# Two weight halves by DMA: a casting load for the rounded half, an accumulating load for the residual

## The chip, the cores and the metric

The kernel runs on one core of a Trainium2 chip. The metric is device time in microseconds of one execution of the whole program, the median of three runs. Below, TensorE is the matrix engine (PE in the profile, with PEld for its weight loads), VectorE is DVE, ScalarE is ACT, GpSimd is POOL and SyncE is SP. DMAs are issued from an engine's queue in the order in which they stand there; those of SyncE go to the hardware queue (q1), those of GpSimd to the software queue (q0).

## The reference

A two-layer decoder trunk for 512 tokens plus 16 learned meta tokens, width 1024, float32. Each sub-layer is `h = LayerNorm(alpha * h + f(h))`:

```
h = concat(meta, x)                                  # 528 tokens
layer 0: h = LN(a*h + gated_deltanet(h));   h = LN(a*h + conv_ffn(h))
layer 1: h = LN(a*h + short_conv_mixer(h)); h = LN(a*h + conv_ffn(h))
conv_ffn(h):         u, gate = split(h @ w_up);  (silu(conv3(u)) * gate) @ w_down     # d_ff 2816
short_conv_mixer(h): b, c, v = split(h @ w_in);  (b * conv3(c * v)) @ w_out
gated_deltanet(h):   q, k, v, z, beta, decay from h @ w_in, conv4 and silu;
                     chunked gated delta rule over 8 heads of 128; RMS norm; * silu(z); @ w_out
```

## The kernel before

Activations lie transposed, 128 channels on the partitions and tokens along the row: `h` holds 8 such slices of 528 tokens. Every large product runs in float32r with both operands in two parts: `hi`, the value rounded to float32r, and `lo`, the rest. A product `W x` is three TensorE products per 128x128 block, `hi*x_hi + hi*x_lo + lo*x_hi` (lines 174 to 176, in `mm_steps`).

Weights come in **strips**: 128 output channels by 1024 (or 768) inputs, a tile of 128 partitions x 1024 numbers, 512 KB. There are 208 of them, in the list `strips` in the order of their use: 24 for q, k and v of the delta net, 8 for its gate z, 8 for its output, then 168 for the first feed-forward (in three parts of 8, 8 and 6 blocks, each an `up` and a `down`), the short convolution (`w_bi`, `w_bo`) and the second feed-forward. `get()` hands out the next strip and first calls `prep` for the strips up to `look` ahead. `prep(i)` allocates a `raw` buffer and a buffer each for `whi` and `wlo`, loads the strip on SyncE's queue into `raw`, and splits it: ScalarE copies `raw` to `whi` with rounding (line 72), VectorE writes `wlo = raw - whi` (line 73). The rings have 4 `raw` buffers (`NR`) and 10 each of `whi` and `wlo` (`NW = (4, 6)`) once the second pool is open; in the delta-net stage 4 and 2. A buffer is written again only when the products that read it are done.

The program is written in one order, and a scheduler sets the final order on each engine's queue; each engine then works its queue strictly in order. The first part (mixer 0, the delta net) weaves the recurrences of the heads with the projections of later heads; there GpSimd also computes (`rk` at 361, `NT` at 380, `R` at 425, `ro` at 494, and others). From the mixer's output projection on (tiles `pd`), TensorE goes through `up` (tiles `pu`), `down` and `short_conv`, with six PSUM banks between it and the engines that empty them: ScalarE copies `pu` to `u` (752), VectorE convolves, ScalarE applies SiLU (756) and the split of the gated result makes `gh` and `gl` (again lines 72 and 73). GpSimd issues eight loads of `x` into `h` at line 568 and then has nothing more to do.

Of the kernel before, what the change touches and what calls it, by code (L numbers as in the profile page):

```python
# [8 lines left out]
F32 = mybir.dt.float32  # L9
# [3 lines left out]
AF = mybir.ActivationFunctionType  # L13
ALU = mybir.AluOpType
PSUM = bass.MemoryType.PSUM

P = 128
D = 1024
KD = D // P
# [38 lines left out]
def tile_hybrid_trunk(ctx, tc, xt, par, cst, msk, w_ba, w_qkv, w_z, w_ao, w_bi, w_bo, w_up, w_dn, out):  # L58
    nc = tc.nc
    V, S, G, TE = nc.vector, nc.scalar, nc.gpsimd, nc.tensor  # L60
# [6 lines left out]
    h = hpool.tile([P, KD, T], F32, name="h")  # L67
# [3 lines left out]
    def split(hi, lo, src):  # L71
        S.activation(hi, src, AF.Copy)  # L72
        V.tensor_tensor(lo, src, hi.bitcast(F32), ALU.subtract)  # L73

# [1 line left out]
    par_sb = cpool.tile([P, NPAR], F32, name="par_sb")  # L76
    cst_sb = cpool.tile([P, NCST], F32, name="cst_sb")
    msk_sb = cpool.tile([P, len(LEVELS), CH], U8, name="msk_sb")
# [8 lines left out]
    nc.sync.dma_start(ba_raw, w_ba)  # L87
    nc.sync.dma_start(h[:, 0, :], xt[:, 0, :])

    # strips of all weights, in the order of their use  # L90
    strips = []

    def add(w, idx, nk=KD, k0=0):
# [12 lines left out]
    SC_LEAD = ((0, 0), (0, 1), (1, 0), (1, 1), (2, 0), (2, 1))  # L106

    def order(nj, parts, lead):
        """(strip, part) in the order of their use."""
        return lead + tuple(x for x in ((j, p) for j in range(nj) for p in range(parts)) if x not in lead)  # L110

    def add_ffn(i):
# [6 lines left out]
    n_gdn = len(strips) - 8  # L119
    add_ffn(0)  # L120
    for j, part in order(8, 3, SC_LEAD):
        add(w_bi, (1, 2, 0)[part] * 8 + j)
# [3 lines left out]

    ready = []
    pools = [wpool]
    NW = (4, 6)
    NR = (2, 2)  # L130
    HOLD6, HOLD8 = 7, 5
    FFN_GRP, SC_GRP = (4, 2), (4, 2)
    STAG = 2
    OUTS = {1: 0, 3: 2, 5: 4, 6: 6, 7: 7}
    UB, CB = 4, 3

    def prep(i):
        src, nk = strips[i]
        x = 0 if i < n_gdn or (i - n_gdn) % sum(NW) < NW[0] else 1
        r = 0 if i < n_gdn + NW[0] or (i - n_gdn - NW[0]) % sum(NR) >= NR[1] else 1  # L140
        raw = pools[r].tile([P, KD, P], F32, name=f"raw{i}", tag="raw", bufs=NR[r])
        hi = pools[x].tile([P, KD, P], F32R, name=f"whi{i}", tag="whi", bufs=NW[x])
        lo = pools[x].tile([P, KD, P], F32R, name=f"wlo{i}", tag="wlo", bufs=NW[x])
        step = nk if i else 4
        for k in range(0, nk, step):
            nc.sync.dma_start(raw[:, k : k + step, :], src[:, k : k + step, :])
        for k in range(0, nk, step):
            split(hi[:, k : k + step, :], lo[:, k : k + step, :], raw[:, k : k + step, :])
        ready.append((hi, lo))

    state = {"next": 0, "look": 3}
# [1 line left out]
    def get():  # L153
# [3 lines left out]
        if len(pools) == 1:  # L157
            end = min(end, n_gdn + NW[0])
        while len(ready) < end:
# [51 lines left out]
    def bcm(ap, n):  # L211
        return ap.unsqueeze(1).to_broadcast([ap.shape[0], n, ap.shape[1]])

    # ================= mixer 0: gated delta net =================
    with ExitStack() as gctx:
        gp = gctx.enter_context(tc.tile_pool(name="gp", bufs=1))
        pm = gctx.enter_context(tc.tile_pool(name="pm", bufs=2, space=PSUM))
# [13 lines left out]
        def gbank(name, tag):  # L231
            return pg.tile([P, 4, P], F32, name=name, tag=tag, bufs=1)

# [1 line left out]
        ba_sb = gp.tile([16, TP], F32, name="ba_sb", tag="ba_sb")  # L235
        V.memset(ba_sb[:, T:], 0.0)
        psba = gtile("psba", 1).rearrange("p (b c) i -> p b (c i)", b=2)
# [11 lines left out]
        beta = cpool.tile([CH, NH, NC_], F32, name="beta")  # L249
# [74 lines left out]
        R5 = range(NC_)  # L324

        def outer(c32, c_hi, c_lo, mat, name, ch, eng):
            """[j, c, i] <- sum_t 1[t > j] mat[t, i] col[t, c]"""
            n = NC_ - 1
            b_hi = gp.tile([CH, n, CH], F32R, name=f"bh{name}", tag="B", bufs=2)
            b_lo = gp.tile([CH, n, CH], F32R, name=f"bl{name}", tag="B", bufs=2)  # L330
            b_32 = gp.tile([CH, CH], F32, name=f"bf{name}", tag="Bf", bufs=2)
            eng.tensor_tensor(b_hi, bcm(mat, n), bc(c_hi[:, :n].bitcast(F32), CH), ALU.mult)
            eng.tensor_tensor(b_lo, bcm(mat, n), bc(c_lo[:, :n], CH), ALU.mult)
            eng.tensor_scalar(b_32, mat, c32[:, n:], None, ALU.mult)
            ps = gtile(f"ps{name}", ch)
            TE.matmul(ps[:CH, :n, :CH], strict_r[:CH], b_hi, start=True, stop=False)
            TE.matmul(ps[:CH, :n, :CH], strict_r[:CH], b_lo, start=False, stop=True)
            TE.matmul(ps[:CH, n, :CH], strict, b_32, start=True, stop=True)
            return ps

        def gdn_a(hd, box, qT, kT, vT, PT):
            """Yields (time of its products, time until what they feed is ready)."""
            ch = hd % 2
            qTv, kTv, vTv = qv(qT), qv(kT), qv(vT)
            small = lambda nm, dt=F32: gp.tile([CH, NC_], dt, name=f"{nm}{hd}", tag=nm, bufs=3)
# [48 lines left out]
            V.tensor_tensor(NT, NT, ps[:CH, :NC_, :CH], ALU.mult)  # L394
            V.tensor_scalar(N16, NT, NSC, None, ALU.mult)
            yield 900, 2200
            # (I - N)^-1 by doubling of the diagonal blocks
            for li in range(len(LEVELS)):
                m_d = bcm(msk_sb[:CH, li, :], NC_)
                p1 = gtile(f"p1{hd}{li}", ch)  # L400
# [19 lines left out]
                S.activation(DT16, pt[:CH, :NC_, :CH], AF.Copy)  # L420
                if not last:
                    yield 250, 1500
            # two correction steps; the residual and its factor in two parts each
            R = full("R")
            G.tensor_tensor(R, D16, bcm(ident16[:CH, :CH], NC_), ALU.subtract)
            yield 250, 2000
# [22 lines left out]
        def gdn_b(hd, box):  # L449
            PT, DT, kd, vb, ssq, nbe, rk, qTv, kTv = (  # L450
                box[x] for x in ("PT", "DT", "kd", "vb", "ssq", "nbe", "rk", "qT", "kT"))
            vn = gp.tile([CH, NC_, P], F32, name=f"vn{hd}", tag="vn")
            oS = gp.tile([CH, NC_, P], F32, name=f"oS{hd}", tag="oS", bufs=1)
            St = gp.tile([P, P], F32, name=f"St{hd}", tag="St")
            rr = gp.tile([CH, P], F32, name=f"rr{hd}", tag="rr")
            sa = gbank(f"sa{hd}", "gb")
            sb = gbank(f"sb{hd}", "gc")
            for c in R5:
                r_ = vb[:, c, :]
                if c > 0:  # L460
                    TE.matmul(sa[:CH, 0, :], kTv[:, c, :], St, start=True, stop=True)
                    TE.matmul(sb[:CH, c - 1, :], qTv[:, c, :], St, start=True, stop=True)
                    V.scalar_tensor_tensor(rr, sa[:CH, 0, :], nbe[:, c : c + 1], vb[:, c, :], ALU.mult, ALU.add)
                    r_ = rr
                    yield 430, 600
                TE.matmul(sa[:CH, 1, :], DT[:, c, :], r_, start=True, stop=True)
                S.activation(vn[:, c, :], sa[:CH, 1, :], AF.Copy, scale=rk[:, c : c + 1])
                yield 220, 800
                if c < NC_ - 1:
                    TE.matmul(sa[:, 2, :], kd[:, c, :], vn[:, c, :], start=True, stop=True)  # L470
                    if c == 0:
                        V.tensor_copy(St, sa[:, 2, :])
                    else:
                        V.scalar_tensor_tensor(St, St, egl[:, hd, c : c + 1], sa[:, 2, :], ALU.mult, ALU.add)
                    yield 220, 800
            V.tensor_tensor(oS[:, 1:, :], sb[:CH], bc(eg[:, hd, 1:], P), ALU.mult)
            yield 0, 500
            ps = gbank(f"po{hd}", "gb")
            for c in range(1, NC_):
                TE.matmul(ps[:CH, c - 1, :], PT[:, c, :], vn[:, c, :], start=True, stop=True)  # L480
            V.tensor_tensor(oS[:, 1:, :], ps[:CH], oS[:, 1:, :], ALU.add)
            ps = gbank(f"po0{hd}", "gc")
            TE.matmul(ps[:CH, 0, :], PT[:, 0, :], vn[:, 0, :], start=True, stop=True)
            S.activation(oS[:, 0, :], ps[:CH, 0, :], AF.Copy)
            # RMS norm, q's length folded into its guard
            sq = gp.tile([CH, P], F32, name=f"sqb{hd}", tag="sqb")
            sso = gp.tile([CH, NC_], F32, name=f"sso{hd}", tag="sso", bufs=2)
            ro = gp.tile([CH, NC_], F32, name=f"ro{hd}", tag="ro", bufs=2)
            for c in R5:
                S.activation(sq, oS[:, c, :], AF.Square, accum_out=sso[:, c : c + 1])  # L490
            V.tensor_scalar(ssq, ssq, L2_EPS, RMS_EPS * P * P, ALU.add, ALU.mult)
            V.tensor_tensor(sso, sso, ssq, ALU.add)
            V.tensor_scalar(sso, sso, 1.0 / P, None, ALU.mult)
            G.tensor_tensor(ro, sso, halfneg[:CH], ALU.pow)
            V.tensor_tensor(oS, oS, bc(ro, P), ALU.mult)
            yield 1080, 0
            box["oS"] = oS
# [87 lines left out]
            pass  # L585

    def warm():
        """Loads the table of the rsqrt ahead of its use."""
        w = lnq.tile([P, 1], F32, name="warm", tag="warm", bufs=1)
        S.activation(w, epsc, AF.Abs_reciprocal_sqrt, bias=epsc)  # L590

# [42 lines left out]
                S.activation(hs, hs, AF.Identity, bias=b_)  # L634

    def down(idx, nk, xh, xl, xoff, s0, first=True, final=True, last=False):
        """h <- alpha h + W x on tokens s0.. (or h + W x), with the norm after the final part."""
        rng = ((s0, SPLIT), (SPLIT, T)) if final or T - s0 > 512 else ((s0, T),)
        acc = [lnq.tile([P, SPLIT], F32, name=f"acc{idx}_{b}", tag=f"lacc{b}")[:, : rng[b][1] - rng[b][0]]
               for b in range(2)] if final else None  # L640
# [45 lines left out]
        lnorm(idx, *rng[1], acc[1], last, last)  # L686

    def up(keys, starts, emit, groups=()):
        """Projections on tokens starts[part].. in two halves, or at once where they fit. groups: the
        numbers of strips to begin with, of which all first halves go before any second half."""  # L690
        sts = {}
        lead = sum(groups)

# [20 lines left out]
        if lead:  # L714
            staggered([go(i, 0) for i in range(lead)])
            i = 0
# [139 lines left out]
```

## Time and profile before

| what | us |
|---|---|
| median of 3 runs (lowest, highest) | 1388.8 (1388.3, 1392.11) |
| span of the profiled execution, first to last instruction | 1386.2 |
| TensorE busy in it | 1350.4 |
| VectorE busy | 804.9 |
| ScalarE busy | 606.2 |
| GpSimd busy | 90.1 |
| mean HBM traffic over the span | 82 GB/s |

The profile is of one execution, with a record for each instruction. A row for a group of instructions gives the source line, the engine, the operation, what it writes and reads, how many there were, their busy time and the mean duration in ns, then the engine's idle time just before them and which instruction ended that wait. Matrix products are pipelined, so the duration of one is longer than the time from one to the next. A DMA's time to landing runs from its issue to the arrival of its data.

### The profile page before, as it was taken

The page shows a single profiled execution, that of the slowest core. Times are in us where ns is not written, and L with a number is a line of the kernel's source. Part 1 is how long each engine was busy: PE and PEld are TensorE (multiplying, and loading weights), DVE is VectorE, ACT ScalarE, POOL GpSimd, SP SyncE. Part 2 cuts the span into 40 slices and gives each one's busy share as a digit, 9 for nine tenths or more (in the row PEclk, how much of TensorE's full clock was granted, in tenths as well). Part 3 has the DMA queues.
Part 4 walks back from the last instruction along what each step waited for, and adds up shares of the span by engine and source line. Part 5 has one row for each costly group of instructions (what it writes and reads, how often), then busy time and mean ns, then how long its engine had stood idle before and what let it go on. Part 6 is the DMA issues. An engine that isn't in the chain of part 4 may idle for free.

```text
span 1386.2 us, 25494 instructions
## 1 busy us (share of the span) xinstructions
PE 1350.4 (97%) x10769; PEld 1288.0 (93%) x10769; DVE 804.9 (58%) x1360; ACT 606.2 (44%) x1218; POOL 90.1 (7%) x132
## 2 busy tenths in 40 slices
PE   8999999999999999999999999999999999999996
PEld 7888998988899999999999999999999889988996
DVE  6767767766469754455344496444775434443436
ACT  6677777676446532233223274222463223322314
POOL 0323322221000000000000000000000000000000
PEclk9999999999999999999999999999999999999999
DMA  5211111211272433233322233333124333322101
GB/s 193 66 58 32 47 32 31 62 32 35 74 244 77 123 93 93 92 94 94 95 79 80 61 107 122 92 92 92 51 87 138 93 97 99 92 92 80 58 1 61
DMA packets 34929, 115.78 MB, mean 84 GB/s; under 512 B 3840, under 2 KB 6400, under 8 KB 34816
## 3 DMA queue, kind: packets, MB, share of 16 engines
q1 hardware_dynamic: 34176, 112.04, 26.3%
q0 software_dynamic: 640, 2.12, 0.4%
q8 instruction: 84, 1.38, 0.4%
q14 instruction: 29, 0.24, 0.1%
HBM read 112.05 MB, written 2.10 MB: 82 GB/s over the span
## 4 chain that ended last, share of the span: by engine, by line
PE 87%; DVE 5%; ACT 4%; issue 2%; POOL 1%; DMA 0%; SPq 0%; ACTq 0%; POOLq 0%; DVEq 0%
PE pu L174 15%; PE pu L175 15%; PE pu L176 15%; PE pd L175 8%; PE pd L174 8%; PE pd L176 8%; PE ps L175 2%; PE ps L174 2%; PE ps L176 2%; DVE acc L316 1%; DVE wlo L73 1%; PE psz L176 1%; PE psz L175 1%; PE psz L174 1%; PE p L403 1%
## 5 line engine op out<-in xcount | busy, mean ns | idle before, releaser
L174 PE MATMUL pu<-hh,whi 128*128 128x258 f32 (+3 forms) x1632 | 477.6, 294 | 1.4 <-ACT hh L632 1.4
L175 PE MATMUL pu<-hl,whi 128*128 128x258 f32 (+3 forms) x1632 | 478.3, 293 | 0.0
L176 PE MATMUL pu<-hh,wlo 128*128 128x258 f32 (+3 forms) x1632 | 477.2, 293 | 0.0
L72 ACT ACTIVATE whi<-raw 128x1024 fp32r<-128x1024 f32 (+2 forms) x209 | 216.7, 1040 | 387.8 <-PE pu L175 168.1
L73 DVE TENSOR_TENSOR wlo<-raw,whi 128x1024 fp32r<-128x1024 f32 (+2 forms) x209 | 249.6, 1196 | 227.0 <-ACT whi L72 224.3
L174 PEld LDWEIGHTS pu<-hh,whi 128*128 128x128 f32 x1632 | 306.8, 188 | 9.1 <-ACT hh L632 1.8
L175 PEld LDWEIGHTS pu<-hl,whi 128*128 128x128 f32 x1632 | 307.3, 188 | 7.5 <-DVE hl L633 0.2
L176 PEld LDWEIGHTS pu<-hh,wlo 128*128 128x128 f32 x1632 | 307.6, 189 | 7.0
L174 PE MATMUL pd<-gh,whi 128*128 128x256 f32 (+3 forms) x704 | 213.4, 303 | 0.0
L175 PE MATMUL pd<-gl,whi 128*128 128x256 f32 (+3 forms) x704 | 212.9, 302 | 0.0
L176 PE MATMUL pd<-gh,wlo 128*128 128x256 f32 (+3 forms) x704 | 212.7, 302 | 0.0
L174 PEld LDWEIGHTS pd<-gh,whi 128*128 128x128 f32 x704 | 132.8, 189 | 5.8
L175 PEld LDWEIGHTS pd<-gl,whi 128*128 128x128 f32 x704 | 132.6, 188 | 5.8
L176 PEld LDWEIGHTS pd<-gh,wlo 128*128 128x128 f32 x704 | 132.7, 188 | 5.7
L174 PE MATMUL ps<-hh,whi 128*128 128x264 f32 x384 | 114.1, 298 | 2.1 <-ACT acc L313 2.1
L176 PE MATMUL ps<-hh,wlo 128*128 128x264 f32 x384 | 115.1, 300 | 0.0
L175 PE MATMUL ps<-hl,whi 128*128 128x264 f32 x384 | 114.6, 298 | 0.0
L174 PEld LDWEIGHTS ps<-hh,whi 128*128 128x128 f32 x384 | 73.4, 191 | 2.6 <-ACT acc L313 2.5
L756 ACT ACTIVATE c<-c 128x516 f32<-128x516 f32 (+1 forms) x44 | 27.6, 632 | 106.8 <-DVE c L727 106.8
L175 PEld LDWEIGHTS ps<-hl,whi 128*128 128x128 f32 x384 | 73.4, 191 | 0.4
L176 PEld LDWEIGHTS ps<-hh,wlo 128*128 128x128 f32 x384 | 73.3, 191 | 0.2 <-DVE wlo L73 0.2
L316 DVE SCALAR_TENSOR_TENSOR acc<-cb,par_sb,acc 128x528 f32<-128x528 f32 x72 | 59.0, 820 | 20.0 <-ACT acc L313 19.6
(228 smaller groups left out, 1865.1 us busy)
## 6 DMA issues: line engine op xcount, KB each, us to landing
raw<-in_w_up_dram SPq DMA_DIRECT2D x88, 512.0 KB, 3.6
raw<-in_w_dn_dram SPq DMA_DIRECT2D x32, 512.0 KB, 3.5
raw<-in_w_bi_dram SPq DMA_DIRECT2D x24, 512.0 KB, 3.6
raw<-in_w_qkv_dram SPq DMA_DIRECT2D x23, 512.0 KB, 3.7
raw<-in_w_dn_dram SPq DMA_DIRECT2D x16, 384.0 KB, 3.1
raw<-in_w_z_dram SPq DMA_DIRECT2D x8, 512.0 KB, 3.6
raw<-in_w_ao_dram SPq DMA_DIRECT2D x8, 512.0 KB, 3.6
raw<-in_w_bo_dram SPq DMA_DIRECT2D x8, 512.0 KB, 3.5
```

The source lines that it names most:

```text
L72: S.activation(hi, src, AF.Copy)
L73: V.tensor_tensor(lo, src, hi.bitcast(F32), ALU.subtract)
L174: TE.matmul(ps, hi[:, k, :], r_h, start=start and k == 0, stop=False)
L175: TE.matmul(ps, hi[:, k, :], r_l, start=False, stop=False)
L176: TE.matmul(ps, lo[:, k, :], r_h, start=False, stop=stop and k == nk - 1)
L316: V.scalar_tensor_tensor(acc, cb[:, t_ : t_ + T], par_sb[:, wo + t_ : wo + t_ + 1], acc, ALU.mult, ALU.add)
L403: TE.matmul(p1[:CH, c, :CH], N16[:, c, :], r_, start=True, stop=True)
L756: S.activation(c, c, AF.Silu)
```

## The change

The strip is loaded twice by GpSimd's queue. `load(i)` issues a casting DMA from the float32 weights straight into `whi` (float32r). `prep(i)` lets ScalarE write the negative of `whi` into `wlo` and then issues an accumulating DMA that adds the float32 weights to `wlo`, which leaves `w - whi` there. `raw` and its four buffers are gone, the rings of `whi` and `wlo` get 5 and 7 buffers, and `load` runs `AHEAD = 2` strips in front of `prep` in the program's order. VectorE has no part in a strip any more. The split of activations (lines 72 and 73) stays.

```diff
-    NW = (4, 6)
-    NR = (2, 2)
+    NW = (5, 7)
+    AHEAD = 2
...
-    def prep(i):
+    loaded = []
+
+    def load(i):
         src, nk = strips[i]
         x = 0 if i < n_gdn or (i - n_gdn) % sum(NW) < NW[0] else 1
-        r = 0 if i < n_gdn + NW[0] or (i - n_gdn - NW[0]) % sum(NR) >= NR[1] else 1
-        raw = pools[r].tile([P, KD, P], F32, name=f"raw{i}", tag="raw", bufs=NR[r])
         hi = pools[x].tile([P, KD, P], F32R, name=f"whi{i}", tag="whi", bufs=NW[x])
         lo = pools[x].tile([P, KD, P], F32R, name=f"wlo{i}", tag="wlo", bufs=NW[x])
         step = nk if i else 4
         for k in range(0, nk, step):
-            nc.sync.dma_start(raw[:, k : k + step, :], src[:, k : k + step, :])
+            nc.gpsimd.dma_start(hi[:, k : k + step, :], src[:, k : k + step, :])
+        loaded.append((hi, lo))
+
+    def prep(i):
+        src, nk = strips[i]
+        while len(loaded) < min(i + 1 + AHEAD, len(strips), n_gdn + NW[0] if len(pools) == 1 else len(strips)):
+            load(len(loaded))
+        hi, lo = loaded[i]
+        loaded[i] = None
+        step = nk if i else 4
         for k in range(0, nk, step):
-            split(hi[:, k : k + step, :], lo[:, k : k + step, :], raw[:, k : k + step, :])
+            S.activation(lo[:, k : k + step, :], hi[:, k : k + step, :].bitcast(F32), AF.Copy, scale=-1.0)
+            nc.gpsimd.dma_start(lo[:, k : k + step, :], src[:, k : k + step, :], accum_op=ALU.add)
         ready.append((hi, lo))
```

In the rows below, a row is an instruction with its source line, its output, its inputs and the output's shape; the lines of the changed program below the edit are 10 higher than those of the one before (174 is 184, 361 is 371, and so on). First TensorE's queue at the very start, before the change (`psba` is the small projection for beta and decay, `ps` the first projection of a head, `whi_87` and `wlo_88` the first strip):

```order
L174 MATMUL psba<-hh,ba_hi 16x264
L175 MATMUL psba<-hl,ba_hi 16x264
L176 MATMUL psba<-hh,ba_lo 16x264
L174 MATMUL ps_305<-hh,whi_87 128x264
L175 MATMUL ps_305<-hl,whi_87 128x264
L176 MATMUL ps_305<-hh,wlo_88 128x264
L174 MATMUL ps_332<-hh,whi_87 128x264
```

And after it, from the fourth product on (the first strip is now `whi_86` and `wlo_87`):

```order
L185 MATMUL psba<-hl,ba_hi 16x264
L186 MATMUL psba<-hh,ba_lo 16x264
L184 MATMUL psba<-hh,ba_hi 16x264
L185 MATMUL ps_307<-hl,whi_86 128x264
L185 MATMUL psba<-hl,ba_hi 16x264
L186 MATMUL psba<-hh,ba_lo 16x264
L184 MATMUL psba<-hh,ba_hi 16x264
L185 MATMUL psba<-hl,ba_hi 16x264
L186 MATMUL psba<-hh,ba_lo 16x264
L185 MATMUL ps_334<-hl,whi_86 128x264
L184 MATMUL psba<-hh,ba_hi 16x264
L186 MATMUL ps_307<-hh,wlo_87 128x264
```

The first product with a residual moved from the 6th place to the 15th, behind products for `psba`.

GpSimd's queue in the delta-net stage, around the fourth head's first operations, before:

```order
L298 TENSOR_TENSOR PT_1623<-PT_1623,cst_sb 106x530
L308 MEMSET cb_2720 128x3
L361 TENSOR_TENSOR rk_1861<-ssk_1859,halfneg 106x5
L332 TENSOR_TENSOR bhE_2160<-cst_sb,gA_hi 106x424
L301 MEMSET qkv_2_3248 128x2
L380 TENSOR_TENSOR NT_1864<-NT_1864,rk_1861 106x530
```

and after:

```order
L146 DMA whi_1768<-in_w_qkv_dram 128x1024
L308 TENSOR_TENSOR PT_1617<-PT_1617,cst_sb 106x530
L318 MEMSET cb_2707 128x3
L371 TENSOR_TENSOR rk_1852<-ssk_1850,halfneg 106x5
L158 DMA wlo_1769<-in_w_qkv_dram 128x1024
L342 TENSOR_TENSOR bhE_2151<-cst_sb,gA_hi 106x424
L311 MEMSET qkv_2_3233 128x2
L390 TENSOR_TENSOR NT_1855<-NT_1855,rk_1852 106x530
L146 DMA whi_2169<-in_w_qkv_dram 128x1024
L343 TENSOR_TENSOR blE_2152<-cst_sb,gA_lo 106x424
L158 DMA wlo_2170<-in_w_qkv_dram 128x1024
```

The casts (line 146) and the accumulates (line 158) now stand among the operations that GpSimd computes.

GpSimd's queue in the first feed-forward, at the start of its second part; before, it held nothing there, and SyncE's queue held one load into `raw` per strip. A `whi` and a `wlo` with the next higher number belong to one strip:

```order
L146 DMA whi_6677<-in_w_up_dram 128x1024
L158 DMA wlo_6678<-in_w_up_dram 128x1024
L146 DMA whi_6778<-in_w_up_dram 128x1024
L146 DMA whi_6835<-in_w_up_dram 128x1024
L158 DMA wlo_6779<-in_w_up_dram 128x1024
L158 DMA wlo_6836<-in_w_up_dram 128x1024
L146 DMA whi_6892<-in_w_up_dram 128x1024
L158 DMA wlo_6893<-in_w_up_dram 128x1024
```

Every accumulate stands behind its own cast, and a strip's cast and accumulate often directly behind each other: of the 168 strips from the first feed-forward on, 99 have no later cast issued ahead of their accumulate, 69 have one to three.

ScalarE's queue in the same part, before (`raw` to `whi`) and after (`whi` to `wlo`):

```order
L72 ACTIVATE whi_7372<-raw_7371 128x1024
L72 ACTIVATE whi_7432<-raw_7431 128x1024
L752 ACTIVATE u_8_7214<-pu_0_0_7189 128x260
L72 ACTIVATE whi_7496<-raw_7495 128x1024
L752 ACTIVATE u_8_7214<-pu_0_1_7216 128x258
L756 ACTIVATE c_8_7242<-c_8_7242 128x516
```

```order
L157 ACTIVATE wlo_7243<-whi_7242 128x1024
L157 ACTIVATE wlo_7306<-whi_7305 128x1024
L762 ACTIVATE u_8_7150<-pu_0_0_7125 128x260
L157 ACTIVATE wlo_7365<-whi_7364 128x1024
L762 ACTIVATE u_8_7150<-pu_0_1_7152 128x258
L766 ACTIVATE c_8_7178<-c_8_7178 128x516
```

The negations took the places of the rounding copies; the copies that empty PSUM stand between them as before.

## The prediction

> **What bounds the kernel now.** I read the busy line of the page first, then the busy time by stage, then what the TensorE queue waits for, then the two lines of the weight split, and last the DMA rows.
>
> ```profile
> span 1386.2 us, 25494 instructions
> PE 1350.4 (97%) x10769; PEld 1288.0 (93%) x10769; DVE 804.9 (58%) x1360; ACT 606.2 (44%) x1218; POOL 90.1 (7%) x132
> core 0: us, PE busy (x) PEld busy (x) DVE busy (x) ACT busy (x) POOL busy (x), PEclk, DMA share, GB/s
> 0.00:20.00 20.00, 14.25 (x84) 11.22 (x84) 9.70 (x22) 10.30 (x19) 2.00 (x21) 1.00 0.65 228
> 20.00:370.00 350.00, 332.74 (x3161) 315.39 (x3160) 245.09 (x427) 239.55 (x620) 83.55 (x103) 1.00 0.17 49
> 370.00:1360.00 990.00, 988.04 (x7422) 947.48 (x7420) 533.03 (x867) 345.08 (x555) 4.55 (x8) 1.00 0.30 93
> 1360.00:1386.00 26.00, 15.39 (x110) 13.94 (x108) 17.09 (x45) 11.28 (x27) 0.00 (x0) 0.93 0.24 81
> ```
>
> TensorE is idle for 5.8 us at the start, 17.3 us in the delta-net stage (20 to 370), 2.0 us in the whole rest up to 1360, and 10.6 us in the last norm. VectorE's 58% hides behind it. So the work that the change removes can pay only where TensorE waits for it:
>
> ```profile
> PE pot L505 <- DVE oS L495: 2.1, 2, 1.7
> ...
> PE psc L281 <- DVE gA L269: 0.3, 1, 0.3
> ```
>
> These are the first and the last of the 12 rows in which TensorE waits for VectorE; together they hold 12.8 us. None names `wlo`. A split does delay TensorE once, at the start: its weight load waits 0.17 us, and the row below is the one to compare with after the change.
>
> ```profile
> 5.64 0.69 DVE L73 TENSOR_TENSOR wlo<-raw,whi 128x512 fp32r<-128x512 f32 x1 [0.23 <-ACT whi L72]
> 6.38 0.29 PEld L176 LDWEIGHTS ps<-hh,wlo 128*128 128x128 f32 x1 [0.17 <-DVE wlo L73]
> L72 ACT ACTIVATE whi<-raw 128x1024 fp32r<-128x1024 f32 (+2 forms) x209 | 216.7, 1040 | 387.8 <-PE pu L175 168.1
> L73 DVE TENSOR_TENSOR wlo<-raw,whi 128x1024 fp32r<-128x1024 f32 (+2 forms) x209 | 249.6, 1196 | 227.0 <-ACT whi L72 224.3
> ```
>
> ScalarE waits for TensorE to give back a `whi` buffer (168 us behind `pu` alone): the weight path runs ahead of its consumer and is throttled by it. That slack is what the change spends.
>
> **Part by part.** *VectorE:* 209 subtractions go, 249.6 us. At the most the 12.8 us above come back, at the least nothing, since those waits are for other results; I take 0, because TensorE's queue never waits for a subtraction after the start.
>
> *ScalarE:* 209 copies of 1.04 us become 209 negations of the same shape and engine, cost 0. What is new is their wait: each stands in ScalarE's queue until a cast has landed, and the copies that empty PSUM (`u`) stand behind it.
>
> *DMA:* one plain load of 512 KB per strip becomes a cast and an accumulate, issued by GpSimd.
>
> ```profile
> q1 hardware_dynamic: 34176, 112.04, 26.3%
> q0 software_dynamic: 640, 2.12, 0.4%
> raw<-in_w_up_dram SPq DMA_DIRECT2D x88, 512.0 KB, 3.6
> L146 SPq DMA_DIRECT2D raw<-in_w_up_dram x88: 327/328/328, 390.9 to 1259.4; - x88
> L146 SPq DMA_DIRECT2D raw<-in_w_dn_dram x48: 327/328/328, 467.9 to 1303.9; - x48
> L568 POOL DMA_DIRECT2D h<-in_xt_dram x8: 546/547/768, 380.0 to 384.9; - x8
> DMA to landing us min/median/max: 3.1/6.7/8.9
> ```
>
> Engine time of a plain strip: 0.263 x 1386.2 x 16 = 5833 engine-us for 112.04 MB, so 0.524 MB takes 27.3, or 1.7 us on 16 engines. The software queue's packets are no dearer (0.004 x 1386.2 x 16 / 640 = 0.14 us each for 3.3 KB, against 5833 / 34176 = 0.17). GpSimd is held 0.55 us by an issue (546 ns). Its fixed part from the end of the issue: the quickest of the eight 259 KB loads landed after 3.1 us, less 0.55, less 0.85 of transfer, leaves 1.7 us. The median of 6.7 has the other seven loads in front and is not a fixed part.
>
> The cast moves as many bytes as the plain load. Between 1.7 us (nothing extra) and 3.4 (the conversion halves the rate) I take 1.7, the row of the same bytes. The accumulate reads the strip and also the tile to which it adds: between 1.7 (the second read is free) and 5.1 (two reads and a write, each a full pass) I take 3.4, one load's time for each stream read, since in the plain load the write is already inside the 1.7. The Trainium skill, DMA: Bandwidth & Descriptors, Rules for kernel authors, states that an accumulating DMA reads its destination and writes it later; no run here shows it yet.
>
> *GpSimd's queue:* this is the path that decides. In the feed-forward and short-convolution part 168 strips (the 88 + 48 + 24 + 8 loads of up, down, `w_bi` and `w_bo`) pass through it, and 99 of them stand as cast and accumulate directly behind each other, with no later cast issued between, as the order rows above show for some. There the accumulate waits for its own negation, that for its own cast, and the next cast stands behind the accumulate in the queue and its bytes behind the accumulate's bytes on the engines. Such a round costs a full chain: the transfers, 1.7 us fixed, 1.06 of ScalarE (the median in the second row below), 0.55 to issue; the other 69 strips only their transfers, because another cast is in flight.
>
> ```profile
> L174 PE MATMUL pd<-hh,whi x128: 274/282/475, 381.4 to 428.5; 128*128 128x262 f32 x64, 128*128 128x256 f32 x64
> L72 ACT ACTIVATE whi<-raw x209: 629/1060/1090, 5.0 to 1324.5; 128x1024 fp32r<-128x1024 f32 x96, 128x768 fp32r<-128x768 f32 x8, 128x512 fp32r<-128x512 f32 x1
> L176 PE MATMUL pd<-gh,wlo x704: 275/282/403, 522.3 to 1370.7; 128*128 128x256 f32 x84, 128*128 128x260 f32 x44, 128*128 128x512 f32 x32, 128*128 128x258 f32 x16
> ```
>
> Queue time: 168 x (1.7 + 3.4) = 857, and 99 x (1.7 + 1.06 + 0.55) = 328; together 1185 us. What it has: the same strips' loads were issued from 390.9 to 1303.9, 913 us, 5.4 a strip. Two more buffers (12 for 10) add two strips of lead, at most 11 us, once; I leave them inside the range. So GpSimd's queue and not TensorE sets the pace.
>
> *Start:* the first two casts are followed in the queue by two whole strips, so the first accumulate's bytes stand behind 2 x 1.7 us, and need 1.7 (half a strip) + 1.7 fixed. After a cast landing near 3.5 and a negation of 0.63 that is 11 to 12 us, against 6.38 for the weight load above. The small `psba` products that moved up cover part. Between 0 and 6 I take 6, since each `psba` product waits in turn for slices of `h`, whose splits stand behind negations.
>
> *Delta-net stage:* GpSimd's own results now stand behind accumulates that wait.
>
> ```profile
> POOL R L425 <- DVE D L415: 36.4, 7, 16.4
> POOL rk L361 <- DVE ssk L360: 25.9, 7, 7.9
> POOL NT L380 <- DVE NT L372: 23.5, 8, 4.0
> ```
>
> These operations already wait 3 to 5 us each time (36.4 / 7, 25.9 / 7, 23.5 / 8), and TensorE's 17.3 us of idle time in this stage are all that comes of it. A round of 1.7 + 3.4 + 3.3 = 8.4 us exceeds them. Between 0 and one round at each of 8 heads (67 us) I take 9, one round uncovered, since the weave gives most of these chains long slack.
>
> *Sum, in the profiled execution:* 390.9 + 15 + 1185 = 1591 for the last accumulate. Behind it: 18 products of the last strip and 144 of the second half, at 988.04 / 7422 = 0.133 us, 21 us, and from the last product to the end 1386.2 - 1370.7 = 15.5. 1628 us in all; the median run, 1388.8, is 2.6 above the profiled span, so 1630. With an accumulate of 2.4 us it is 1460, and with 5.1 it is 1915.
>
> **The rivals.** *A, the transfers overlap and the accumulate costs no more than a plain load.* Then 168 x 3.4 + 328 = 899, just under 913: TensorE sets the pace again, and start and delta-net stage stay: 1404, a little more where full rounds come in a row (3.4 + 3.3 = 6.7 us against 5.4), so 1410. For it: the 16 DMA engines stand at a share of 0.30 in the stage that counts (windows above). Against it: two reads where there was one. The Trainium skill, DMA: Bandwidth & Descriptors, Anatomy of one DMA, fits software DMAs by 2.0 us + bytes / 436 GB/s; by that a strip's transfer is 1.2 us, the queue's time by an estimate from that page 168 x 2.4 + 99 x 3.6 = 760, and the outcome is this rival's. By that fit 259 KB would land in 2.6 us, and the trace's quickest is 3.1.
>
> *B, not slower.* One mechanism: VectorE, freed of 249.6 us, serves TensorE's 12 kinds of waits earlier, in the delta-net stage. Place: 20 to 370. Price: at most 12.8 us back, less the 6 of the start, so 1382. It decides only if the queue keeps up: 168 e + 328 < 913, that is both transfers together under 3.5 us, and if none of GpSimd's results come late. The 0.17 us that TensorE ever waited for `wlo` speak against it.
>
> *C, converting and adding run at half the rate or less:* 3.4 and 5.1 us. Then 168 x 8.5 + 328 = 1756, and 391 + 15 + 1756 + 37 + 3 = 2200. Nothing in this trace shows such a transfer, so nothing excludes it.
>
> *D, the cast rounds nothing and the residual is zero:* then the same instructions still run, and the time is one of the above.
>
> **How the numbers follow.** My forecast, the accumulate between 2.4 and 5.1 us, has 0.62: 1460 to 1915, likeliest 1630. A has 0.16, B 0.08, C 0.14. The range leaves out B and most of C: 1400 to 2000. About 0.3%, 4 us, is what a measurement of this kernel can tell from no change. Slower has 0.62 + 0.14 + nearly all of A: 0.90. B splits between faster, 0.05, and same, 0.05 with a sliver of A.
>
> **What would show it.** Right: TensorE idle by about 240 us, spread over the feed-forward part, ended by `wlo` from the DMA; ScalarE's negations waiting for the cast; GpSimd's queue waiting for ScalarE about 100 times; VectorE near 555 us busy; the software queue near 214 MB (twice the weights); the first `wlo` product at 11 to 12 us; the first product of the mixer's output projection (381.4 before, first row of that fence) 10 to 20 us later. Wrong: an accumulate that lands in the time of a plain load, TensorE again 97% busy, or DMA engines near full share with GpSimd's queue never waiting for ScalarE, which would be C rather than the chain.

## The result, and the profile after

| | median us (lowest to highest) | ratio to before [95% interval] |
|---|---|---|
| before | 1388.6 (1387.5 to 1392.1) | |
| after | 1587.3 (1583.0 to 1592.1) | 1.1423 [1.1393, 1.1452] |

The kernel became 199 us slower; 1630 us was forecast, between 1400 and 2000. The fence holds the busy line of the page of the kernel after, its busy time by stage (same columns as before), its software queue, and its granted clock in 40 slices.

```profile
span 1590.3 us, 25623 instructions
PE 1414.4 (89%) x10769; PEld 1335.1 (84%) x10769; DVE 580.0 (36%) x1151; ACT 595.7 (37%) x1218; POOL 384.1 (24%) x550
0.00:20.00 20.00, 9.09 (x37) 6.35 (x38) 5.84 (x14) 9.76 (x15) 7.18 (x17) 1.00 0.97 278
20.00:400.00 380.00, 353.57 (x3282) 332.66 (x3280) 219.13 (x404) 240.93 (x630) 125.96 (x180) 0.99 0.42 90
400.00:1560.00 1160.00, 1032.29 (x7327) 978.62 (x7327) 335.57 (x683) 331.88 (x546) 250.96 (x353) 0.94 0.67 156
1560.00:1590.00 30.00, 19.43 (x130) 17.49 (x128) 19.41 (x52) 13.09 (x30) 0.00 (x0) 0.83 0.21 71
q0 software_dynamic: 60832, 216.06, 59.4%
PEclk9999999999999999998999899998999999979998
```

TensorE does the same 10769 products, but it is idle for 1590.3 - 1414.4 = 176 us instead of 36. Its busy time has grown too, from 1350.4 to 1414.4, because the granted clock is lower (0.94 where it was 1.00). The DMA engines carry twice the bytes and are still only 0.67 busy in the stage that counts, so their bytes alone are not the limit.

What each engine waited for: the engine and the line of its instruction, whom it waited for, microseconds, times, longest.

```profile
POOL wlo L158 <- ACT wlo L157: 587.6, 133, 8.9
ACT wlo L157 <- DMA whi<-in_w_up_dram: 325.8, 68, 9.6
POOL wlo L158 <- ACT u L762: 208.9, 40, 9.5
POOL whi L146 <- PE pu L186: 65.5, 11, 22.3
PE pd L184 <- ACT gh L72: 45.1, 8, 13.3
PE pu L184 <- ACT u L762: 43.1, 16, 5.4
PE ps L186 <- DMA wlo<-in_w_qkv_dram: 2.3, 1, 2.3
```

The accumulate (158) waits on GpSimd for ScalarE's negation, and the negation (157) waits for the cast. TensorE waits for ScalarE's copies (`u`, `gh`), which stand in ScalarE's queue behind such negations. It waits for the residual itself for 2.5 us in all, 2.3 of them at the start. The rhythm is seen in the timeline of the kernel after, first GpSimd, then ScalarE (start, duration, instruction, idle time before it and what ended that):

```profile
1102.13 0.85 POOL L158 DMA_DIRECT2D wlo<-in_w_up_dram  x1 [6.83 <-ACT wlo L157]
1102.68 0.87 POOL L146 DMA_DIRECT2D whi<-in_w_up_dram  x1
1111.15 0.85 POOL L158 DMA_DIRECT2D wlo<-in_w_up_dram  x1 [7.60 <-issue]
...
1108.90 1.06 ACT L157 ACTIVATE wlo<-whi 128x1024 fp32r<-128x1024 f32 x1 [6.54 <-issue]
```

An accumulate is issued at 1102.1, the next cast right behind it at 1102.7; its negation runs from 1108.9, and only then can the next accumulate go, at 1111.15. This round takes 9.0 us, somewhat more than its neighbours, where TensorE needs a strip every 5.4 (before, 913 us for 168 strips). In the whole trace 68 of the 168 strips go through such a full round, in which the queue holds an accumulate, the next strip's cast and that strip's accumulate directly behind each other. A round takes 8.3 us in the median and 8.5 on average, 577 us together. The other 31 of the 99 strips that have no later cast ahead of their accumulate stand in groups that share one wait, mostly two casts and then their two accumulates; the 23 groups of that form take 10.4 us on average, 5.2 a strip.

The first products with a residual, the first and last products of the two groups that bound the stages (`pd<-hh,whi` opens the output projection, the last `pd<-gh,wlo` closes the last `down`), and the landing time of casts and accumulates:

```profile
L186 PE MATMUL ps<-hh,wlo x384: 278/285/589, 14.8 to 311.0; 128*128 128x264 f32 x192
L184 PE MATMUL pd<-hh,whi x128: 274/282/476, 402.5 to 458.0; 128*128 128x262 f32 x64, 128*128 128x256 f32 x64
L186 PE MATMUL pd<-gh,wlo x704: 275/282/632, 553.3 to 1573.0; 128*128 128x256 f32 x84, 128*128 128x260 f32 x44, 128*128 128x512 f32 x32, 128*128 128x258 f32 x16
L158 POOL DMA_DIRECT2D wlo<-in_w_dn_dram x48: 844/857/892, 506.9 to 1533.4; - x48
DMA to landing us min/median/max: 3.7/6.4/12.8
...
DMA to landing us min/median/max: 4.7/5.7/13.8
```

From these rows, and the same two of each other kernel's trace, the span splits into three stages: up to the output projection, from there to the last `down` product, and the tail. The table gives, for each profiled execution, by how much a stage is longer than before (381.4, 989.3 and 15.5 us):

| kernel | first stage | middle | tail | span |
|---|---|---|---|---|
| after | +21.1 | +181.2 | +1.8 | 1590.3 |
| ring | +10.3 | +4.8 | +1.8 | 1403.1 |
| ring1 | +17.4 | +20.1 | +0.1 | 1423.8 |
| cast | +4.0 | +10.1 | 0.0 | 1400.3 |
| acc | +7.2 | +9.8 | 0.0 | 1403.2 |
| negpool | +16.2 | +413.9 | +1.8 | 1818.1 |
| ffn | +2.5 | +200.2 | +1.7 | 1590.6 |
| gdn | +24.9 | 0.0 | +1.7 | 1412.8 |
| start | +5.4 | 0.0 | +0.3 | 1391.9 |
| ringold | +3.3 | +15.9 | +1.8 | 1407.2 |
| late | -0.9 | +7.6 | +1.7 | 1394.6 |

Of the 204 us between the two spans, 181 lie in the middle stage.

### The profile page after: what moved, and what is told of

Same layout as the page of the kernel before. It is cut to its first block, busy times and chain, and to the rows that moved or that the text cites. A ratio compares the mean times of both kernels' runs of the same rounds, so it can differ in the third digit from the quotient of the medians.

```text
span 1590.3 us, 25623 instructions
## 1 busy us (share of the span) xinstructions
PE 1414.4 (89%) x10769; PEld 1335.1 (84%) x10769; DVE 580.0 (36%) x1151; ACT 595.7 (37%) x1218; POOL 384.1 (24%) x550
## 4 chain that ended last, share of the span: by engine, by line
issue 50%; PE 19%; POOL 14%; DMA 8%; ACT 5%; DVE 3%; SPq 0%; POOLq 0%; ACTq 0%; DVEq 0%
POOL whi L146 7%; POOL wlo L158 6%; DMA whi<-in_w_qkv_dram 2%; PE pd L185 1%; PE pd L184 1%; PE pd L186 1%; PE pu L184 1%; PE pu L185 1%; PE pu L186 1%; ACT wlo L157 1%; PE ps L185 1%; PE ps L184 1%; PE ps L186 1%; DMA whi<-in_w_up_dram 1%; DMA par_sb<-in_par_dram 1%
## 5 line engine op out<-in xcount | busy, mean ns | idle before, releaser
L184 PE MATMUL pu<-hh,whi 128*128 128x258 f32 (+3 forms) x1632 | 491.3, 301 | 54.0 <-ACT u L762 43.1
L157 ACT ACTIVATE wlo<-whi 128x1024 fp32r<-128x1024 f32 (+2 forms) x209 | 216.6, 1037 | 719.5 <-DMA whi<-in_w_up_dram 325.8
L184 PEld LDWEIGHTS pu<-hh,whi 128*128 128x128 f32 x1632 | 317.8, 195 | 66.5 <-ACT u L762 46.8
L185 PEld LDWEIGHTS pu<-hl,whi 128*128 128x128 f32 x1632 | 318.1, 195 | 7.6 <-DVE hl L643 0.5
L184 PE MATMUL pd<-gh,whi 128*128 128x256 f32 (+3 forms) x704 | 224.2, 318 | 62.2 <-ACT gh L72 45.1
L158 POOL DMA_DIRECT2D wlo<-in_w_up_dram x88 | 77.0, 875 | 391.9 <-ACT wlo L157 290.2
L735 DVE TENSOR_SCALAR c<-u,par_sb 128x516 f32<-128x516 f32 (+1 forms) x44 | 21.6, 491 | 273.7 <-ACT u L762 273.7
L158 POOL DMA_DIRECT2D wlo<-in_w_dn_dram x48 | 41.4, 862 | 260.0 <-ACT wlo L157 131.8
L73 DVE TENSOR_TENSOR gl<-c,gh 128x516 fp32r<-128x516 f32 (+1 forms) x44 | 30.4, 694 | 182.1 <-ACT gh L72 182.1
L146 POOL DMA_DIRECT2D whi<-in_w_up_dram x88 | 66.2, 805 | 55.0 <-PE pu L186 41.8
```

Source lines behind the costliest of these rows:

```text
L146: nc.gpsimd.dma_start(hi[:, k : k + step, :], src[:, k : k + step, :])
L157: S.activation(lo[:, k : k + step, :], hi[:, k : k + step, :].bitcast(F32), AF.Copy, scale=-1.0)
L158: nc.gpsimd.dma_start(lo[:, k : k + step, :], src[:, k : k + step, :], accum_op=ALU.add)
L184: TE.matmul(ps, hi[:, k, :], r_h, start=start and k == 0, stop=False)
L185: TE.matmul(ps, hi[:, k, :], r_l, start=False, stop=False)
L735: V.tensor_scalar(dst, src[:, 0:n], par_sb[:, off : off + 1], None, ALU.mult)
```

## The experiments

Three theories stood at the outset. Theory 1 is the prediction's: rounds in GpSimd's in-order queue, where an accumulate stands directly behind its own cast. Theory 2: twice the bytes and a dear accumulate fill the DMA engines. Theory 3: the negations in ScalarE's queue hold back the copies that empty PSUM.

### ring: more casts ahead, same bytes

```diff
-    NW = (5, 7)
-    AHEAD = 2
+    NWH = (6, 8)    # whi: 14 buffers, allocated in load
+    NWL = (4, 6)    # wlo: 10 buffers, allocated in prep
+    AHEAD = 4
```

It has the 24 buffers of after, dealt out otherwise. In after a strip's two buffers come free together, and the schedule often puts its cast and its accumulate directly behind each other (68 of the 168 later strips); 99 have no later cast issued ahead of their accumulate. In ring there are four more `whi` than `wlo`, and 163 of the 168 have four. (The place of the allocation has no part in it: with 12 and 12 the queue of the built program has the order of after, 99 included; that program was not run.)

> Edit: 14 whi and 10 wlo buffers instead of 12 and 12, so that four casts stand ahead of each accumulate in GpSimd's queue (163 of 168 strips instead of 4 with three or more); bytes and instructions unchanged. Theory 1, the chain (an accumulate directly behind its own cast costs a full round of cast, negation and issue): the 99 rounds vanish, the queue's time falls to the transfers, 168 x 4.6 = 773 us against 913, and only the start and the delta-net stage stay (about 21 us): 1400 to 1415 us. Theory 2, bytes (the DMA engines, at a share of 0.67, are the limit): 1570 to 1600. Theory 3, ScalarE's queue (a negation that waits for a cast holds the copies out of PSUM): the casts have landed by then, so 1400 to 1415 too.

Measured: 1406.3 us, ratio 1.0123 [1.0108, 1.0138]. The lines show the stage from 400 to 1370 us of ring, then two of its waits.

```profile
400.00:1370.00 970.00, 964.81 (x7221) 923.88 (x7220) 329.33 (x666) 325.75 (x523) 240.74 (x339) 1.00 0.83 182
...
POOL whi L160 <- PE pu L213: 358.4, 92, 23.1
POOL wlo L184 <- ACT wlo L183: 150.8, 149, 5.7
```

TensorE is busy for 964.8 of 970 us and its clock is back at 1.00. GpSimd now waits mostly for TensorE to give back a `whi` buffer, as ScalarE did before the change. All the bytes, casts, accumulates and negations are still there: 182 of the 199 us went with the other order, for the same 24 buffers. The same bytes pass in less time, at a DMA share of 0.83, so Theory 2 falls. Theory 3 is not decided by this run: ScalarE does the same negations, but their casts have landed by then, and it expected the same time.

### ring1: one cast ahead, with one buffer fewer than after

```diff
-    NWH = (6, 8)
-    NWL = (4, 6)
-    AHEAD = 4
+    NWH = (5, 7)
+    NWL = (5, 6)
+    AHEAD = 2
```

The diff is against ring. It tells the order apart from the number of buffers: 12 `whi` and 11 `wlo`, against 12 and 12 in after, with the same `AHEAD = 2`. 128 of the 168 strips have one later cast ahead of their accumulate, 36 have two, 3 three, and one none.

> Edit: one wlo buffer fewer than the changed kernel (12 whi, 11 wlo), so that one cast stands ahead of each accumulate (none of the 168 strips but the last is left with its own cast directly ahead of it, 99 before); less memory, same bytes and instructions. Theory 1 (the full round is the cost): one cast in flight during the wait hides most of cast and fixed part, so 1410 to 1440, near the 1406 of four casts ahead. Theory 3 (ScalarE's queue): the negation still waits for a cast issued one round earlier and still stands ahead of the copies; if holding them were the cost, 1480 to 1560. A smaller ring alone, without the order, would make it slower than 1587.

Measured: 1426.2 us, ratio 1.0266 [1.0249, 1.0282]. One cast in flight beside the round, for one buffer less, is worth 161 us; four are worth 20 more. This lies in the range of Theory 1 and below the 1480 to 1560 of Theory 3, though the negations still stand in ScalarE's queue ahead of the copies. What shrank is their wait for a cast, here for those of `w_up` (325.8 us in after):

```profile
ACT wlo L183 <- DMA whi<-in_w_up_dram: 104.4, 36, 6.2
```

This is the plainest evidence for Theory 1.

### acc and cast: half of the change each

```diff
 acc, load:   nc.sync.dma_start(raw, src)
 acc, prep:   S.activation(hi, raw, AF.Copy)
              S.activation(lo, hi, AF.Copy, scale=-1.0)
              nc.gpsimd.dma_start(lo, src, accum_op=ALU.add)
 cast, load:  nc.sync.dma_start(raw, src)
              nc.gpsimd.dma_start(hi, src)
 cast, prep:  V.tensor_tensor(lo, raw, hi, ALU.subtract)
```

In acc the rounding stays on ScalarE and only the residual comes by an accumulating DMA. In cast the residual is VectorE's subtraction and only the rounding comes by DMA. Both have the rings of before.

> Edit: the cast is undone, the accumulate stays: raw comes by SyncE's queue, ScalarE rounds it to whi and writes the negative, GpSimd accumulates; buffers as before the change, one ScalarE copy of 1.04 us more per strip. Theory 1: loads run ahead on SyncE's queue, so an accumulate waits only for its negation and nothing stands behind it but the next accumulate: 1400 to 1430. Theory 2: the bytes of the changed kernel still move, 168 x 4.6 us, so 1570 to 1600. Theory 3: two ScalarE copies per strip, but their loads have landed: 1400 to 1430. The accumulate's own engine time is read from the software queue's share, about 3.1 us per 512 KB.

> Edit: the accumulate is undone, the cast stays: raw comes by SyncE's queue, whi by GpSimd's casting DMA, VectorE subtracts as before the change; buffers as before the change. Theory 1: no accumulate, no rounds, GpSimd's queue holds only casts that wait for buffers: 1388 to 1400, the rest being a later start. Theory 2: 1.0 MB per strip still moves in, 168 x 2 x 1.5 = 504 us of engine time, no limit: 1388 to 1400. Theory 3: no negation on ScalarE: 1388 to 1400, and ScalarE's idle time in front of weight work gone. The cast's own engine time is read from the software queue's share: 1.45 to 1.7 us per 512 KB if converting costs nothing.

Measured: acc 1404.8 us, ratio 1.0115 [1.0098, 1.0133]; cast 1401.6 us, ratio 1.0093 [1.0076, 1.011]. acc lies where Theories 1 and 3 put it, far below the range of Theory 2; cast lies 1.6 us above the range that all three theories shared, so it tells nothing between them. Neither half has the dear round, since in each the two loads of a strip stand in different queues or only one of them must wait. The queue rows (packets, MB, share of the 16 engines' span) give the prices that the prediction had to bound: first acc, then cast.

```profile
q0 software_dynamic: 30736, 109.09, 45.4%
q1 hardware_dynamic: 34176, 112.04, 24.6%
```

```profile
q0 software_dynamic: 30736, 109.09, 25.5%
q1 hardware_dynamic: 34176, 112.04, 24.6%
```

By the prediction's working, an accumulate of 0.524 MB takes 0.454 x 1403.2 x 0.524 / 109.09 = 3.06 us of all 16 engines, a cast 0.255 x 1400.3 x 0.524 / 109.09 = 1.72, and a plain load beside it 0.246 x 1400.3 x 0.524 / 112.04 = 1.61. A cast costs hardly more than a plain load, an accumulate 1.8 times a cast. The price fits what the Trainium skill, DMA: Bandwidth & Descriptors, Rules for kernel authors, states, that an accumulate reads its destination and writes it later; no trace here shows that read by itself.

### negpool: the negations off ScalarE

```diff
-    S.activation(lo, hi, AF.Copy, scale=-1.0)
+    G.tensor_scalar(lo, hi, -1.0, None, ALU.mult)   # from the output projection on
```

Otherwise it is built like after: `AHEAD = 2`, 12 buffers of each, and again 68 of the 168 accumulates directly behind their own cast (93 with no later cast ahead of them). If ScalarE's queue were the cause, this would free it.

> Edit: from the output projection on, GpSimd instead of ScalarE writes the negative of whi into wlo; DMAs, buffers and bytes unchanged. Theory 1: the rounds stay, 93 accumulates still stand behind their own cast, and each strip costs GpSimd a negation of 2 to 3 us (from 1.49 us for 106x530) that ScalarE did in 1.06: slower than the changed kernel, 1650 to 1850. Theory 3: no weight work stands in ScalarE's queue, the 118 us in which TensorE waits for ScalarE's copies vanish: 1420 to 1480. Theory 2: 1570 to 1600.

Measured: 1819.3 us (two runs), ratio 1.3096 [1.3069, 1.3122]. The first line is the group of GpSimd's negations, with what ended the waits ahead of them, the second the largest of five such waits of TensorE, 283 us together.

```profile
L186 POOL TENSOR_SCALAR wlo<-whi 128x1024 fp32r<-128x1024 f32 (+1 forms) x176 | 512.5, 2929 | 583.7 <-DMA whi<-in_w_up_dram 298.7 <-DMA whi<-in_w_dn_dram 150.6 <-DMA whi<-in_w_bi_dram 43.8
...
PE pu L216 <- DMA wlo<-in_w_up_dram: 125.9, 36, 8.8
```

ScalarE is free of them and the kernel is slower still, because a negation takes 2.93 us on GpSimd instead of 1.04 and lies in the same round. The 68 full rounds take 10.1 us in the median, 1.8 more than in after, which is about what the negation grew by. So the round, not ScalarE's load, sets the pace. The second line also bears on the kernel after: there TensorE was stopped by `u` and `gh`, here by the residual itself. The waits behind ScalarE in after were the round seen through ScalarE's queue.

### gdn and ffn: the change in one stage only

```diff
+    def mode(i):
+        return 'dma' if i < n_gdn else 'old'     # gdn: strips of the delta net's projections only
+        return 'old' if i < n_gdn else 'dma'     # ffn: the strips behind them only
```

Here `n_gdn` is 32; the rings are those of before, 10 and 10. In ffn 70 of the 168 accumulates stand directly behind their own cast (101 with no later cast ahead of them).

> Edit: the new scheme in the first 32 strips (start and delta-net stage) alone, the old one (load by SyncE, VectorE's subtraction) in the other 176. Theory 1: what was seen at the first product of the output projection, 402.5 against 381.4, is this part's cost, so 1388 + 15 to 21: 1402 to 1410. If the late start of that projection came from the strips behind the delta net, 1390 to 1396.

> Edit: the old scheme in the first 32 strips, the new one from the output projection on, with 10 and 10 buffers; 101 of 168 accumulates directly behind their own cast. Theory 1: the whole loss but that of the start and the delta net: 1587 - 21 = 1566, and up to 20 more or less for two strips of lead less and one or two rounds more: 1550 to 1600.

Measured: gdn 1412.2 us, ratio 1.0168 [1.0149, 1.0187]; ffn 1592.3 us, ratio 1.1465 [1.1446, 1.1485]. gdn came 2 us above the range expected of it, ffn within its own. The middle stage of gdn is as long as before to 0.1 us, that of ffn is 200 us longer. The two parts, +24 and +204, do not add up to after's +199. Two reasons are likely, neither tried alone: ffn has two buffers fewer of each kind, and a late start is partly taken up by a queue that paces the rest anyway.

### start: the first three strips only

```diff
+    def mode(i):
+        return 'dma' if i < 3 else 'old'
```

> Edit: the new scheme in the first 3 strips alone. Theory 1, the start term (the first residual needs a cast, a negation and an accumulate one after the other, behind two other strips and the slices of h): 1388 + 5 to 9, so 1393 to 1398. If TensorE makes up for the late start in the delta net, where its recurrences have slack: 1388 to 1391.

Measured: 1392.1 us over 11 runs, ratio 1.0022 [1.0013, 1.0031]. The residual comes late here too (its first product at 13.5 us, 6.4 before), but of these 7 us only 3.5 reach the end. The expectation of the smaller loss lies below this value and that of the larger one above, so neither is met.

### ringold and late: what is left of the cost

```diff
 ringold: 'old' for the first 32 strips, then NWH = (4, 9), NWL = (4, 5), AHEAD = 4
 late:    'old' for the first 72 strips, then NWH = (4, 7), NWL = (4, 5), AHEAD = 2
```

ring keeps 17 us. These two ask whether they come from the first stage, and whether VectorE's free time brings anything once the order is right.

> Edit: the old scheme in the first 32 strips, the new one behind them with 13 whi and 9 wlo buffers and four casts ahead: neither the late start nor the rounds are left, and VectorE is free of 176 subtractions. Theory 1: TensorE is busy without a gap there with or without VectorE's subtractions, so no gain and no loss but at the change of scheme: 1385 to 1400. A rival, that VectorE's freed time serves norms and convolutions earlier: below 1384.

> Edit: the old scheme in the first 72 strips, the new one in the other 136, with 11 whi and 9 wlo buffers and two casts ahead: the change of scheme comes in the middle of the first feed-forward, where no output projection waits. What the run with the old scheme in the first 32 strips left open (1409 instead of 1385 to 1400): if its 20 us came from filling the rings while the output projection already drew on them, 1386 to 1394 here; if the new scheme slows TensorE wherever it runs, by about 12 us in 918 as it seemed there, 1397 to 1402. VectorE is free of 136 subtractions; a gain from that would be under 1384.

Measured: ringold 1408.9 us, ratio 1.014 [1.012, 1.0161], which is a miss: by the table of stages, 7 us came back in the first stage (+3.3 for ring's +10.3), but 11 more went in the middle one. late 1397.6 us, ratio 1.0064 [1.005, 1.0078], in the range that was expected if the new scheme slows TensorE wherever it runs. The fence has two stretches of ringold, then the second of them in before, and 702 to 902 us of late.

```profile
381.00:440.00 59.00, 53.37 (x416) 52.06 (x416) 28.22 (x68) 29.34 (x50) 25.68 (x39) 0.97 1.02 278
440.00:1300.00 860.00, 852.09 (x6367) 816.75 (x6366) 281.69 (x565) 289.14 (x463) 211.82 (x300) 1.00 0.84 184
...
440.00:1300.00 860.00, 858.63 (x6427) 822.45 (x6426) 452.57 (x711) 292.06 (x459) 0.00 (x0) 1.00 0.31 93
...
702.00:902.00 200.00, 195.95 (x1612) 194.69 (x1612) 79.42 (x174) 71.60 (x124) 50.96 (x71) 0.99 0.79 178
```

Where the scheme sets in, many buffers are filled at once: the DMA share is at 1.02 from 381 to 440 us, and TensorE is idle 5.6 us of the 59. That is a part of the miss. Behind it TensorE still loses 6.5 us in 860 against before, and in late about 3 in 200 (before is busy for 198.6 us from 700 to 900). With only the last 136 strips changed, late's middle stage is 7.6 us longer. What this small loss is, with the order right and the DMA engines 0.8 busy, was not settled: the two halves, acc and cast, have it as well (+9.8 and +10.1).

No version ran faster than before.

## Why the prediction was right, and where it was not

**GpSimd's queue sets the pace: right.** The part from the first `up` cast (416.6 us) to the last accumulate (1533.4) took 1117 us; 1185 were forecast, and the old loads had 913. ring and ring1 show that the order in that queue carries the loss.

**99 full rounds: too many.** The prediction took all 99 strips with no later cast ahead of their accumulate for full rounds. 68 are; the rest share a wait, as `wlo_6779` and `wlo_6836` do in the queue shown with the change, behind the casts of both. Of the 1117 us, the 68 rounds took 577, and the other 100 strips 540, 5.4 each.

**The cast at 1.7 us: right, measured 1.72. The accumulate at 3.4: too high, measured 3.06.** With this term the prediction's own sum gives 168 x (1.72 + 3.06) + 99 x 3.31 = 1131 us, 14 from the 1117 measured; the 1591 for the last accumulate become 1537. The closeness is partly luck: that sum charges 99 rounds of 8.1 us and 4.8 for each other strip, where the trace has 68 rounds of 8.5 and 5.4 for each other strip.

**Fixed part 1.7 us.** The quickest cast landed after 3.7 us, which leaves 3.7 - 0.55 - 1.72 = 1.4, so the term was about right. By the Trainium skill, DMA: Bandwidth & Descriptors, Anatomy of one DMA, an estimate for 512 KB is 2.0 + 1.2 = 3.2 us; after has 3.7 at the least and 6.4 in the median, with other transfers in flight.

**What TensorE waits for: wrong in form.** Idle time of about 240 us, ended by `wlo` from the DMA, was forecast. It was 176 us, 128 of them from 400 to 1560 us, and of these the copies of ScalarE (`u`, `gh` and the short convolution's `bc`) ended 111. The prediction had named that those stand behind waiting negations, but gave the wait to the wrong row. It did not foresee that TensorE itself would run slower: 64 us more busy time at a clock of 0.953 for 0.999.

**Start and delta net: 21 us for 15.** The first residual product came at 14.8 us, not 11 to 12 (6.4 before): the first negation began at 5.5 instead of 3.5, and the accumulate issued at 6.4 took 8.4 us to land, in the first 20 us, in which the DMA share is 0.97. But the kernel start, with three strips changed, has its output projection only 5.4 us later, so the 6 us of the sum were about right. From 20 us to that projection TensorE is idle for 27.0 us (17.8 before), which is 9 us more, the size that the sum had for this stage. Of the 6.5 us that are left, three stretches of 3.4 us at half the clock account for at most 5, by an estimate; that the clock would fall was not foreseen.

**Tail: too small.** From the last accumulate to the last product 39.6 us, and 17.3 to the end: 57 for 37.

```profile
1533.40:1573.00 39.60, 35.79 (x292) 34.90 (x292) 27.09 (x64) 11.47 (x26) 0.89 (x1) 1.00 0.15 37
1573.00:1590.30 17.30, 6.43 (x21) 4.55 (x19) 8.12 (x21) 6.91 (x17) 0.00 (x0) 0.70 0.18 62
```

The step counted 162 products behind the last accumulate; 292 were left when it was issued, and 277 when it had landed, 5.0 us later. The clock is full there and falls only in the norm behind the last product, which takes 1.8 us longer. So the forecast came near by errors that cancel in part: in the profiled execution the queue took 68 us less than its sum, it began 11 us later (416.6 for 405.9), and 20 us more lay behind it, which makes 1590 of the 1628.

**VectorE: right that it brings nothing.** Its busy time is 580.0, not 555: the groups add up to 855.1 us before and 608.3 after, which is the subtraction's 249.6 to within 3 us, but some 50 of the 855.1 had overlapped. Rival B needs a kernel whose queue keeps up and whose VectorE is freed in the delta-net stage. ring and acc are such, and their first stages are 10.3 and 7.2 us longer than before. ringold and late, which free VectorE only behind that stage, are not faster either.

**Rivals.** A needed an accumulate as cheap as a plain load: it costs 1.8 to 1.9 times as much. C needed half the rate: cast 1.72 against 3.4, accumulate 3.06 against 5.1. With D the time would be the same; it does not come into it. Of the smaller signs, the software queue moved 216 MB, as was said, and from the first `up` cast on the accumulates waited for ScalarE 162 times, not about 100.

## What to carry to other kernels

When two dependent DMAs of one item go through one in-order queue with another engine's step between them, count in the schedule how many of the second stand directly behind the first: each costs a full round (8.3 us in the median here, for 4.8 us of transfers), and one later load issued ahead of the wait hides most of it (1587 to 1426 us). Rings of unequal depth did that, one buffer fewer for the second step than for the first. And before work is taken off an engine, see whether anyone waits for that engine: 250 us less on VectorE were worth nothing here, even with the queue mended.

## What the runs showed of the hardware

A casting DMA costs the engines about as much as a plain one (1.72 against 1.61 us for 512 KB), an accumulating one 3.06. The record of an issue on GpSimd lasts 0.53 to 0.55 us for plain loads and for casts alone, and about 0.86 for an accumulate. The fence has the casts and the accumulates of after, then the accumulates of acc, where no cast is in the queue:

```profile
L146 POOL DMA_DIRECT2D whi<-in_w_up_dram x88: 527/864/1067, 416.6 to 1470.2; - x88
L158 POOL DMA_DIRECT2D wlo<-in_w_up_dram x88: 844/870/1112, 427.0 to 1478.9; - x88
...
L184 POOL DMA_DIRECT2D wlo<-in_w_up_dram x88: 863/863/884, 411.6 to 1299.3; - x88
```

A cast of after that stands directly behind an accumulate mostly has the longer record too (0.87 us in the median), and one that comes after a pause has 0.55. The longer record does not hold up the next issue: in the timeline above the cast starts 0.55 us after the accumulate (1102.13 and 1102.68), while the accumulate's record still runs. Why it is longer was not tried.

The granted clock fell as TensorE's idle time grew: 0.999, 0.996, 0.953 and 0.906 at 36, 45, 176 and 353 us of idle time (before, ring, after, negpool). The Trainium skill, TensorE: Matmul & The Clock Gate, HAM oscillation, states that idle gaps over some 3.4 us lower the clock; the runs agree in direction, with waits of 45.1 / 8 = 5.6 us for `gh` in after, but none was made to isolate it. In the trace of after the clock is either full or half, at half in 29 stretches of about 150 us together. Of these, 14 have an idle gap of TensorE of 3.4 us or more within the 7 us ahead of them, the others only shorter ones, so the rule alone does not account for them. By an estimate, half of the 150 us is the most that this can add to the busy time, which grew by 64; how much of that lay on the path stays open.
